# Two-layer diffusion block on one core: the Fourier and gate stage with VectorE in program order

## The chip, the cores and the metric

The kernel runs on one NeuronCore of one Trainium2 chip. The metric is device time in microseconds of one execution. Five engines work in parallel: TensorE (PE in the profile; PEld is its weight load), VectorE (DVE), ScalarE (ACT), GpSimd (POOL) and SyncE (SP), whose queue issues most of the DMAs. Each engine runs its own instructions in order and waits on semaphores for the others.

## The reference, cut to what matters

The input is 1024 latent tokens of width 1024 and 256 context tokens. Layer 0 (the even layer) computes a modulated RMSNorm `h`, one combined projection, and from it two mixers side by side: four Fourier channel groups and four heads of differential attention. Both are multiplied by a SiLU gate and go through one output projection. Layer 1 is a gated short convolution. Shift, scale and gate of each layer are the adaLN columns `silu(c) @ ada_w + ada_b`.

```python
def fourier_mix(u):
    u32 = u.reshape(b, n, F_GROUPS, F_CH).astype(jnp.float32)
    f = jnp.fft.fftn(u32, axes=(1, 3), norm="ortho").real
    return f.reshape(b, n, F_WIDTH)

proj = h @ w_in                       # F | Q | K | V | G
y = concatenate([fourier_mix(proj[F]), rms_norm(attn_o) * (1 - lam_init)]) * silu(proj[G:])
x_lat = x_lat + gate * (y @ w_out)
```

## The kernel before, in words

Every matmul that needs fp32 accuracy is run as three: each operand is split into a rounded part `hi` and a rest `lo`, and hi x hi, hi x lo and lo x hi are summed. ScalarE rounds (`nc.scalar.copy`), VectorE or GpSimd subtracts (function `part`, lines 61 and 62).

**Who sets the order.** A kernel written in this way has its instructions ordered by a planner ahead of time. Inside `manual_schedule(engines={...})` the engines named keep the order of the program text; the others are placed by the planner, which follows the text as a priority and starts an instruction early when its inputs and its buffer are there. From line 555 on only TensorE is in text order; VectorE, ScalarE, GpSimd and the SP queue are the planner's. Tiles come from pools: tiles with the same tag share `bufs` buffers. In the pool `post`, the tag "o" has four buffers and serves `vo` (line 606), `ko` (line 327) and the running sums `ada_sum` (line 564).

**The projections, lines 593 to 660.** `proj_tok(tt, c)` makes one tile of 128 tokens x 512 columns with 24 matmuls of 512 columns. The loops run over K (c = 0), V (c = 1, ten tiles, tt = 0 to 9), Q (c = 2, eight tiles, tt = 2 to 9) and three of the Fourier tiles (c = 3). In this text V3 is the V tile with tt = 3, and so on. Each Q tile is post-processed by `qk_norm`, `qk_scaled` and `qk_a`: a square on ScalarE (L307), a sum on VectorE (L309), two small instructions on GpSimd (L310, L311), then VectorE: `kn` (L316), the two halves of `ko` (L332), L334 and `od` (L340). `od` is transposed by TensorE inside a later tile.

**The adaLN columns beside them.** Eight columns (two of layer 0, six of layer 1) are made in this phase; the text calls them sum 1 to sum 8. `ada_m(half)` takes four 128 x 512 blocks of weights of one half and adds them, each scaled by silu(c), to `ada_sum`: half 0 allocates the sum, and asks for the next column's two loads of 1 MB into three buffers; half 1 finishes it and puts it on the list `sums`. All eight steps of a sum are one chain, each reading what the one before wrote. In the V loop all steps are VectorE's (L579 for the first, L576 for the others). In the Q loop the last two of each half are scaled by ScalarE (L573) and added by GpSimd (L574). `ada_step(n)` takes the latest entry off `sums` when n is odd, and its four matmuls with a column of ones (L586) run in the next `proj_tok` ahead of its last step, k = 7. TensorE is in order, so it waits there for the sum. In the V loop half 0 is called at even tt and half 1 at odd tt; in the Q loop the same. Sum 6 is begun after Q2, finished after Q3 and used in Q5; sums 7 and 8 follow two tiles apart.

**The Fourier stage, lines 664 to 766.** The 512 Fourier columns of the eight token tiles are folded by sums and differences (lines 689 to 705, VectorE), split into the big tiles `arena` (lines 706 to 708), and transformed over tokens per channel group g by `fft_a(g)` (lines 720 to 743: 30 matmuls, then three splits on ScalarE and VectorE) and over channels by `fft_b(g)` (lines 745 to 765: 9 matmuls, a copy `mid`, a copy `fee`, a sum and a difference into `fo`).

**The gates, lines 788 to 911.** The first two gate columns are made by `gate_half(f, half)`, a full tile of 24 matmuls. The other six are made two at a time (groups g = 0, 1, 2) with seven products instead of eight (Strassen's scheme, in Winograd's form): `gop(g, p)` prepares the weight operand, `gate_product(g, p)` runs 12 matmuls into one of the PSUM banks X, Y, Z. Products 5, 6 and 4 need sums and differences of the tokens: `g_diff` (lines 837 to 842) makes `tk[k] = H1[k] - H0[k]` in three steps, `g_less` subtracts it again, `t3` makes H1[k] - H1[k+4]. Of the four k of each, three are VectorE's and one GpSimd's (`GE`, line 854). Product 7 adds onto the bank that product 6 filled, and product 4 onto that of 7, each after ScalarE has copied the bank out.

The text order before is: gate tile (0,1), `fft_a(0)`, then three times [gate tile, `fft_b`, `fft_a`], the products (0,1) and (1,1), the last `fft_b`, then 19 products in the list `order`. Attention follows: its loads into `arena` wait for products 5 and 6 of group 2, and its first score matmul (L982) takes over the PSUM banks of the last products.

Of the kernel before, what the change touches and what calls it, by code (L numbers as in the profile page):

```python
# [8 lines left out]
F32 = mybir.dt.float32  # L9
# [28 lines left out]
def block_kernel(tc, A):  # L38
# [550 lines left out]
    def ada_step(n):  # L589
        if n % 2 and sums:  # L590
            cols.append(lambda a=sums.pop(): ada_c(*a))
# [87 lines left out]
    fx = opn("fx", "right")  # L679


    for n in range(2):
        eo = []
        for m in (n, n + 2):
            psa = pf.pop(0) if pf else proj_tok(NTC + m, 3)
            a = fx.tile([P, NB], F32, name="fa", bufs=1)
            nc.scalar.copy(out=a, in_=psa)
            psb = pf.pop(0) if pf else proj_tok(NTC + m + 4, 3)
            for i, op in enumerate((ALU.add, ALU.subtract)):
                e = fx.tile([P, NB], F32, name=f"fe{i}", bufs=2)  # L690
                nc.vector.tensor_tensor(out=e, in0=a, in1=psb, op=op)
                eo.append(e)
        ea, oa, eb, ob = eo
# [12 lines left out]
        for (h, l), u in zip(EO, us):  # L706
            nc.scalar.copy(out=h[:, n, :], in_=u)
            nc.vector.tensor_sub(out=l[:, n, :], in0=u, in1=f32(h[:, n, :]))
    cls("fx")
# [35 lines left out]
    def fft_b(g, ch, cl, sh, sl, dh, dl):  # L745
# [4 lines left out]
        for pp, a, b, i, n in ((p6, dh, dl, 0, 2), (pe, ch, cl, 0, NB), (po, sh, sl, 2, NB)):  # L750
# [37 lines left out]
    def gate_half(f, half):  # L788
# [7 lines left out]
        gate_out(f, half, ge.tile([P, NB], F32, name="sg", bufs=2), ps)  # L796
# [15 lines left out]
    def gate_product(g, p):  # L812
# [6 lines left out]
        new = lambda: go.tile([P, NB], F32, name="go", bufs=5) if go else ge.tile([P, NB], F32, name="sg", bufs=2)  # L819
# [15 lines left out]
    tk = []  # L835

    def g_diff(t, k, a, b, eng):

        x, y = H[a][k[0]], H[b][k[1]]
        tt = lambda i, j, op: eng.tensor_tensor(out=t, in0=i, in1=f32(j), op=op)  # L840
        tt(f32(x[0]), y[0], ALU.subtract)
        tt(t, x[1], ALU.add)
        tt(t, y[1], ALU.subtract)

    def g_less(k, half, eng):
# [8 lines left out]
    GE = (nc.vector, nc.vector, nc.vector, nc.gpsimd)  # L854
    def t3():
        for k in range(4):
            u = v0[:, hsl[k % 2]]
            g_diff(u, (k, k + 4), 1, 1, GE[k])
            nc.scalar.copy(out=H[1][k][0], in_=u)
            GE[k].tensor_tensor(out=H[1][k][1], in0=u, in1=f32(H[1][k][0]), op=ALU.subtract)  # L860

# [3 lines left out]
    for i in range(2):  # L865
        tk += halves(wp.tile([P, T], F32, name="tk", tag="wraw", bufs=2))
    for k in range(4):
        g_diff(tk[k], (k, k), 1, 0, GE[k])
# [12 lines left out]
    gate_product(1, 1)  # L881
    fft_b(*cur)
# [3 lines left out]
    qs = [quarter_of(t) for t in (*arena, t4)]  # L886
    GB.update({5: [(q[:, 0, :], q[:, 1, :]) for q in qs[0]], 6: [(q[:, 0, :], q[:, 1, :]) for q in qs[1]],
               4: [(q[:, 0, :], q[:, 1, :]) for q in qs[2]]})
    for k in range(4):
        part(tk[k], qs[0][k], GE[k])  # L890
    gop(0, 6)
    for k in range(4):
        g_less(k, 1, GE[k])
        part(tk[k], qs[1][k], GE[k])
    gop(0, 2)
    gop(0, 7)
    gop(1, 5)
    for k in range(4):
        g_less(k, 0, GE[k])
        part(tk[k], qs[2][k], GE[k])  # L900
    order = [(0, 5), (0, 6), (0, 2), (0, 7), (1, 5), (0, 4), (1, 6), (0, 3), (1, 7), (1, 2),
             (2, 1), (1, 4), (2, 5), (2, 6), (1, 3), (2, 7), (2, 2), (2, 4), (2, 3)]
    ahead = order[5:]
    for n, (g, p) in enumerate(order):
        if ahead:
# [4 lines left out]
        gate_product(g, p)  # L910
# [706 lines left out]
```

## Time and profile before

| | |
|---|---|
| three runs, us | 1132.86, 1139.51, 1139.52 (median 1139.51) |
| the profiled execution, us | 1135.15 |
| its span, us | 1133.4 |
| mean granted TensorE clock | 0.974 of full speed |
| projections K, V, Q and Fourier tiles on TensorE | about 23 to 279.7 us |
| Fourier and gate stage on TensorE | 279.7 to 396.6 us |

Times in the views are microseconds from the start of the span. A row of the timeline gives start, duration, engine, line, operation, output <- inputs, shapes and count; in brackets, how long the engine had been idle before it and which instruction ended that. The view of windows gives, for stretches of the span, the busy time of each engine, the mean granted clock of TensorE, and the DMA share. The busy time of a matmul is longer at a lower clock, so idle time and clock both have to be counted.

### The profile page before, as it was taken

To read this page: it belongs to the slowest core of one execution; us is meant where nothing else is said; L and a number is where in the kernel's file an instruction comes from. 1 tells how busy PE (TensorE), PEld (TensorE's weight loads), DVE (VectorE), ACT (ScalarE), POOL (GpSimd) and SP (SyncE) were. 2 spreads that over 40 slices of the span, in tenths; PEclk is the share of its full clock that TensorE was granted. 3 is DMA by queue.
4 is the path that set the end of the run, shared out by engine and by line. 5 is a ranking of instruction groups with operands and counts; after the bars stand their busy time and mean duration, and the time that the engine had idled before them with its cause. 6 is when DMAs were issued, how large, how long until landed. Compare 5 with 4: busy or idle time off the path is not lost.

```text
span 1133.4 us, 14135 instructions
## 1 busy us (share of the span) xinstructions
PE 1043.9 (92%) x5118; PEld 851.1 (75%) x5118; DVE 763.0 (67%) x1073; ACT 480.0 (42%) x868; POOL 498.8 (44%) x422
## 2 busy tenths in 40 slices
PE   4989899989888989999999998889999999998598
PEld 2657688778777878999988876568888888776486
DVE  4599856874868178888873287985645554578642
ACT  4453123311443367777763363633333333343320
POOL 1257103631556236676575455654343444332331
PEclk9999899989899999999999999989999999999799
DMA  9724895434020795271004541121111111111421
GB/s 346 295 94 131 267 296 182 145 112 159 9 93 26 181 262 133 79 182 47 21 20 165 198 165 50 37 75 38 67 46 56 56 57 56 56 67 55 166 76 65
DMA packets 61381, 131.12 MB, mean 116 GB/s; under 512 B 5248, under 2 KB 30208, under 8 KB 58112
## 3 DMA queue, kind: packets, MB, share of 16 engines
q1 hardware_dynamic: 60240, 125.64, 34.8%
q0 software_dynamic: 1072, 4.59, 1.1%
q8 instruction: 40, 0.66, 0.2%
q14 instruction: 29, 0.24, 0.1%
HBM read 105.57 MB, written 24.64 MB: 115 GB/s over the span
## 4 chain that ended last, share of the span: by engine, by line
PE 54%; DVE 16%; POOL 3%; ACT 3%; issue 3%; DMA 3%; SPq 0%; ACTq 0%; DVEq 0%; POOLq 0%
PE psX L649 6%; PE psX L650 6%; PE psX L651 6%; PE ps_av L1032 5%; PE psY L649 3%; PE psY L650 3%; PE psY L651 3%; PE S L982 3%; PE S L983 2%; PE ps_t L1022 2%; DVE nm L987 2%; PE ps_feat L1085 2%; PE ps_feat L1087 2%; PE ps_feat L1086 2%; DVE arena L62 2%
## 5 line engine op out<-in xcount | busy, mean ns | idle before, releaser
L61 ACT CAST wop<-wraw 128x512 fp32r<-128x512 f32 x152 | 93.3, 620 | 130.6 <-PE psY L651 28.0
L62 POOL TENSOR_TENSOR wop<-wraw,wop 128x512 fp32r<-128x512 f32 x72 | 99.7, 1388 | 76.8 <-ACT wop L61 76.4
L284 PE MATMUL ps_tok<-whi,hhi 128*128 128x512 f32 x288 | 119.0, 413 | 3.4 <-ACT hhi L393 2.5
L285 PE MATMUL ps_tok<-whi,hlo 128*128 128x512 f32 x288 | 115.7, 402 | 4.3 <-DVE hlo L397 4.2
L286 PE MATMUL ps_tok<-wlo,hhi 128*128 128x512 f32 x288 | 114.8, 399 | 0.0
L987 DVE TENSOR_REDUCE nm<-S 128x1 f32<-128x1280 f32 x64 | 95.0, 1487 | 22.1 <-PE S L983 20.0
L649 PE MATMUL psX<-B,wop 128*128 128x512 f32 x240 | 97.3, 405 | 9.8 <-ACT c L1293 4.9
L998 ACT ACTIVATE p<-S,nm 128x1280 f32<-128x1280 f32 x64 | 85.2, 1332 | 44.6 <-DVE nm L987 38.9
L650 PE MATMUL psX<-B,wop 128*128 128x512 f32 x240 | 96.9, 404 | 1.5 <-POOL B L1439 1.1
L651 PE MATMUL psX<-B,wop 128*128 128x512 f32 x240 | 96.4, 402 | 0.5 <-POOL wop L62 0.5
L628 POOL TENSOR_TENSOR s<-wraw 128x512 f32<-128x512 f32 x20 | 27.3, 1363 | 120.0 <-DMA wraw<-in_wodd_dram 114.0
L62 DVE TENSOR_TENSOR wop<-wraw,wop 128x512 fp32r<-128x512 f32 x80 | 68.9, 863 | 13.2 <-ACT wop L61 12.9
L628 POOL TENSOR_TENSOR wraw<-wraw 128x512 f32<-128x512 f32 x40 | 56.6, 1421 | 47.9 <-DVE wop L62 40.4
L1032 PE MATMUL ps_av<-v,aT 128*128 128x128 f32 x640 | 76.8, 275 | 0.0
L1032 PEld LDWEIGHTS ps_av<-v,aT 128*128 128x128 f32 x640 | 74.2, 192 | 0.2
L285 PEld LDWEIGHTS ps_tok<-whi,hlo 128*128 128x128 f32 x288 | 55.5, 193 | 18.8 <-DVE hlo L397 8.0
L1009 POOL TENSOR_TENSOR p<-p,cc 128x256 f32<-128x256 f32 x32 | 40.4, 1262 | 65.6 <-DVE cc L1006 46.6
L284 PEld LDWEIGHTS ps_tok<-whi,hhi 128*128 128x128 f32 x288 | 55.7, 193 | 17.8 <-ACT hhi L393 3.7
L649 PE MATMUL psY<-B,wop 128*128 128x512 f32 x160 | 64.1, 400 | 3.6 <-DVE u L1301 1.8
L650 PE MATMUL psY<-B,wop 128*128 128x512 f32 x160 | 64.2, 401 | 0.6 <-POOL B L1439 0.3
L286 PEld LDWEIGHTS ps_tok<-wlo,hhi 128*128 128x128 f32 x288 | 55.4, 192 | 11.9
L651 PE MATMUL psY<-B,wop 128*128 128x512 f32 x160 | 63.7, 398 | 0.0
(344 smaller groups left out, 2671.7 us busy)
## 6 DMA issues: line engine op xcount, KB each, us to landing
ada_raw<-in_ada_dram SPq DMA_DIRECT2D x24, 1024.0 KB, 6.6
wraw<-in_wodd_dram SPq DMA_DIRECT2D x32, 512.0 KB, 3.5
wraw<-in_wo_dram SPq DMA_DIRECT2D x24, 512.0 KB, 3.8
wraw<-in_wtok_dram SPq DMA_DIRECT2D x16, 512.0 KB, 4.2
arena<-kd SPq DMA_DIRECT2D x16, 320.0 KB, 8.6
kq<-kd SPq DMA_DIRECT2D x16, 320.0 KB, 9.7
xt<-in_xT_dram SPq DMA_DIRECT2D x16, 256.0 KB, 5.8
xr<-in_xT_dram SPq DMA_DIRECT2D x16, 256.0 KB, 3.8
```

The lines of the kernel that those rows point to most:

```text
L61: nc.scalar.copy(out=o[:, 0, :], in_=src)
L62: eng.tensor_tensor(out=o[:, 1, :], in0=src, in1=f32(o[:, 0, :]), op=ALU.subtract)
L284: nc.tensor.matmul(ps, lhsT=hh, rhs=whi, start=k == 0, stop=False)
L285: nc.tensor.matmul(ps, lhsT=hl, rhs=whi, start=False, stop=False)
L286: nc.tensor.matmul(ps, lhsT=hh, rhs=wlo, start=False, stop=k == KT - 1)
L628: tt = lambda out, x, y, op: nc.gpsimd.tensor_tensor(out=out, in0=x, in1=y, op=op)
L649: nc.tensor.matmul(ps, lhsT=a, rhs=x[k][0], start=start and k == 0, stop=False, skip_group_check=not start)
L650: nc.tensor.matmul(ps, lhsT=a, rhs=x[k][1], start=False, stop=False, skip_group_check=not start)
L651: nc.tensor.matmul(ps, lhsT=b, rhs=x[k][0], start=False, stop=k == 3, skip_group_check=not start)
L987: nc.vector.tensor_reduce(out=nm, in_=S[m][:, :NKEY], op=ALU.max, axis=AX.X, negate=True)
L998: nc.scalar.activation(out=p, in_=S[m][:, :NKEY], func=AF.Exp, bias=tiles.pop((i, m, "nm")), accum_out=z)
L1032: nc.tensor.matmul(ps, lhsT=groups[i, k // 4][:, (k % 4) * P:(k % 4 + 1) * P], rhs=v[:, k * P:(k + 1) * P], start=k == 0, stop=k == NK - 1)
```

## The change

1. **The order of VectorE.** After the third Fourier tile of the projections the `manual_schedule` is closed and opened again with TensorE and VectorE. So in the whole Fourier and gate stage VectorE runs in text order, and the text is rearranged for that: roundings on ScalarE run one step ahead of the subtractions on VectorE (`lagged`).
2. **Token differences on VectorE alone.** `g_diff`, `g_less`, `t3` and the splits of the `tk` lose their engine argument; GpSimd's quarter of them goes to VectorE. The `tk` differences move to the head of the stage, between the Fourier tiles.
3. **Two gate tiles ahead of the first transform.** (0,1) and (1,1) come before `fft_a(0)`; the remaining two gate tiles and the two first products lie between the transforms.
4. **Products reordered,** so that a product that adds onto a bank seldom follows directly on the one that is copied out of it; operands are prepared four products ahead, after the product, where it was five, ahead of it.
5. **Buffers.** `fa` and `fee` use halves of `v0`; `mid` is copied by ScalarE; the tag "sg" has three buffers instead of two, and odd steps of `t3` use the tag "s1".
6. **The adaLN columns one tile later.** In the V loop `ada_m` begins at tt = 1 with half 0, so halves 0 fall on odd tt; the Q loop continues with half 1 of sum 5 at tt = 2. `ada_step` now takes a sum when its argument is even, and the Q loop calls it with tt + 1. Followed through by hand, sums 1, 2 and 3 are used in V4, V6 and V8 (before: V3, V5, V7). Sums 5 to 8 are still used in Q3, Q5, Q7 and Q9. Sum 6 is begun after Q3 and finished after Q4 (before: after Q2 and Q3), sums 7 and 8 likewise one tile later. Sum 4 stays on the list until the second Fourier tile (before: V9).

```diff
     def ada_step(n):
-        if n % 2 and sums:
+        if n % 2 == 0 and sums:
             cols.append(lambda a=sums.pop(): ada_c(*a))
...
         ps = proj_tok(tt, 1, (4,))
-        ada_m(tt % 2)
+        if tt:
+            ada_m((tt + 1) % 2)
...
-        ada_step(tt)
+        ada_step(tt + 1)
         fins.append(qk_a(proj_tok(tt, 2, (5,)), 0, tt))
-        ada_m(tt % 2, 2)
+        ada_m((tt + 1) % 2, 2)
...
     pf = []
-    ada_step(1)
     for m in (0, 4, 2):
         qk_b(*fins.pop(0))
+        if m == 4:
+            ada_step(0)
         pf.append(proj_tok(NTC + m, 3, (5,)))
...
+    man.__exit__(None, None, None)
+    man = tc.manual_schedule(engines={ENG.PE, ENG.DVE})
+    man.__enter__()
...
+            if m == 1:
+                g_diff(tk[2], (2, 2), 1, 0)
+                g_diff(tk[3], (3, 3), 1, 0)
...
+        if n == 0:
+            g_diff(tk[0], (0, 0), 1, 0)
+            g_diff(tk[1], (1, 1), 1, 0)
...
             if n == 2:
-                nc.vector.tensor_copy(out=mid, in_=p6[:, 0:2])
-        e = fev.tile([P, NB], F32, name="fee", bufs=1)
+                nc.scalar.copy(out=mid, in_=p6[:, 0:2])
+        e = v0[:, 0:NB]
...
     gate_half(0, 1)
+    gate_half(1, 1)
+    t3((0, 1))
     cur = fft_a(0)
-    for g, fh in ((1, (1, 1)), (2, (0, 0)), (3, (1, 0))):
-        gate_half(*fh)
-        fft_b(*cur)
-        cur = fft_a(g)
-        if g == 1:
-            t3()
-            gop(0, 1)
-            gop(1, 1)
-            gop(0, 5)
+    t3((2, 3))
+    gate_half(0, 0)
+    gop(0, 1)
+    gop(1, 1)
+    fft_b(*cur)
+    cur = fft_a(1)
+    gate_half(1, 0)
+    gop(0, 5)
+    gop(0, 2)
+    fft_b(*cur)
+    cur = fft_a(2)
     gate_product(0, 1)
+    gop(1, 5)
+    fft_b(*cur)
+    cur = fft_a(3)
     gate_product(1, 1)
+    gop(1, 2)
+    qs = [quarter_of(t) for t in arena]
+    tpart(qs[0], range(4))
     fft_b(*cur)
...
-    order = [(0, 5), (0, 6), (0, 2), (0, 7), (1, 5), (0, 4), (1, 6), (0, 3), (1, 7), (1, 2),
-             (2, 1), (1, 4), (2, 5), (2, 6), (1, 3), (2, 7), (2, 2), (2, 4), (2, 3)]
-    ahead = order[5:]
+    tpart(qs[1], range(4), 1)
+    order = [(0, 5), (0, 2), (1, 5), (1, 2), (0, 6), (1, 6), (0, 7), (1, 7), (0, 4), (0, 3), (1, 4), (1, 3),
+             (2, 1), (2, 5), (2, 6), (2, 2), (2, 7), (2, 4), (2, 3)]
+    ahead = order[4:]
     for n, (g, p) in enumerate(order):
+        gate_product(g, p)
+        if n in (2, 3):
+            tpart(qs[2], (2 * n - 4, 2 * n - 3), 0)
         if ahead:
             q = ahead.pop(0)
             gop(*q)
             if q[1] == 3:
                 gload(q[0] + 2)
-        gate_product(g, p)
```

`tpart(q, ks, half)` does for each k: `g_less` if a half is given (two subtractions), the rounding on ScalarE, and one step later the subtraction of the rest on VectorE.

More of the change, by code (lines that the diff above doesn't have):

```diff
@@ L679, in block_kernel, with g_diff @@
     fx = opn("fx", "right")
+    tk = []
+    for i in range(2):
+        tk += halves(wp.tile([P, T], F32, name="tk", tag="wraw", bufs=2))
+    def g_diff(t, k, a, b):
+        x, y = H[a][k[0]], H[b][k[1]]
+        tt = lambda i, j, op: nc.vector.tensor_tensor(out=t, in0=i, in1=f32(j), op=op)
+        tt(f32(x[0]), y[0], ALU.subtract)
+        tt(t, x[1], ALU.add)
+        tt(t, y[1], ALU.subtract)
     for n in range(2):
@@ L685, in block_kernel @@
             psa = pf.pop(0) if pf else proj_tok(NTC + m, 3)
-            a = fx.tile([P, NB], F32, name="fa", bufs=1)
+            a = v0[:, NB:T]
             nc.scalar.copy(out=a, in_=psa)
@@ L795, in gate_half @@
             nc.tensor.matmul(ps, lhsT=b, rhs=H[half][k][0], start=False, stop=k == KT - 1)
-        gate_out(f, half, ge.tile([P, NB], F32, name="sg", bufs=2), ps)
+        gate_out(f, half, ge.tile([P, NB], F32, name="sg", bufs=3), ps)
     graws, gops, gdone, gbanks, gouts = {}, {}, set(), {}, {}
@@ L818, in gate_product @@
         f = 2 + 2 * g
-        new = lambda: go.tile([P, NB], F32, name="go", bufs=5) if go else ge.tile([P, NB], F32, name="sg", bufs=2)
+        new = lambda: go.tile([P, NB], F32, name="go", bufs=5) if go else ge.tile([P, NB], F32, name="sg", bufs=3)
         if p in (1, 6):
@@ L833, in gate_product, with g_less @@
             gate_out(f + 1, 0, new(), X)
[L835 to L845, printed above, removed]
+    def g_less(k, half):
         x = H[half][k + 4]
-        eng.tensor_tensor(out=tk[k], in0=f32(x[0]), in1=tk[k], op=ALU.subtract)
-        eng.tensor_tensor(out=tk[k], in0=tk[k], in1=f32(x[1]), op=ALU.add)
+        nc.vector.tensor_tensor(out=tk[k], in0=f32(x[0]), in1=tk[k], op=ALU.subtract)
+        nc.vector.tensor_tensor(out=tk[k], in0=tk[k], in1=f32(x[1]), op=ALU.add)
     def quarter_of(t):
@@ L853, in block_kernel, with lagged, rounded, rest @@
     GB = {1: H[0][:4], 2: H[0][4:], 3: H[1][4:], 7: H[1][:4]}
[L854 to L860, printed above, removed]
+    def lagged(steps):
+        held = None
+        for a, b in steps:
+            r = a()
+            if held:
+                held()
+            held = lambda b=b, r=r: b(r)
+        held()
+    def rounded(src, hi):
+        nc.scalar.copy(out=hi, in_=src)
+    def rest(src, hi, lo):
+        nc.vector.tensor_tensor(out=lo, in0=src, in1=f32(hi), op=ALU.subtract)
+    def t3(ks):
+        def a(k):
+            u = ge.tile([P, NB], F32, name="s1", bufs=1) if k % 2 else v0[:, NB:T]
+            g_diff(u, (k, k + 4), 1, 1)
+            rounded(u, H[1][k][0])
+            return u
+        lagged([(lambda k=k: a(k), lambda u, k=k: rest(u, *H[1][k])) for k in ks])
+    def tpart(q, ks, half=None):
+        def a(k):
+            if half is not None:
+                g_less(k, half)
+            rounded(tk[k], q[k][:, 0, :])
+        lagged([(lambda k=k: a(k), lambda _, k=k: rest(tk[k], q[k][:, 0, :], q[k][:, 1, :])) for k in ks])
     go = None
@@ L864, in block_kernel @@
     gload(1)
[L865 to L868, printed above, removed]
     gate_half(0, 1)
+    gate_half(1, 1)
+    t3((0, 1))
     cur = fft_a(0)
-    for g, fh in ((1, (1, 1)), (2, (0, 0)), (3, (1, 0))):
-        gate_half(*fh)
-        fft_b(*cur)
-        cur = fft_a(g)
-        if g == 1:
-            t3()
-            gop(0, 1)
-            gop(1, 1)
-            gop(0, 5)
+    t3((2, 3))
[9 more added lines that the diff above has]
+    cur = fft_a(2)
     gate_product(0, 1)
+    gop(1, 5)
+    fft_b(*cur)
+    cur = fft_a(3)
     gate_product(1, 1)
+    gop(1, 2)
+    qs = [quarter_of(t) for t in arena]
+    tpart(qs[0], range(4))
     fft_b(*cur)
@@ L885, in block_kernel @@
     t4 = go.tile([P, 8 * NB], F32R, name="t4")
[L886 to L900, printed above, removed]
-    order = [(0, 5), (0, 6), (0, 2), (0, 7), (1, 5), (0, 4), (1, 6), (0, 3), (1, 7), (1, 2),
-             (2, 1), (1, 4), (2, 5), (2, 6), (1, 3), (2, 7), (2, 2), (2, 4), (2, 3)]
-    ahead = order[5:]
+    qs.append(quarter_of(t4))
+    for p, q in zip((5, 6, 4), qs):
+        GB[p] = [(t[:, 0, :], t[:, 1, :]) for t in q]
+    tpart(qs[1], range(4), 1)
+    order = [(0, 5), (0, 2), (1, 5), (1, 2), (0, 6), (1, 6), (0, 7), (1, 7), (0, 4), (0, 3), (1, 4), (1, 3),
+             (2, 1), (2, 5), (2, 6), (2, 2), (2, 7), (2, 4), (2, 3)]
+    ahead = order[4:]
     for n, (g, p) in enumerate(order):
+        gate_product(g, p)
+        if n in (2, 3):
+            tpart(qs[2], (2 * n - 4, 2 * n - 3), 0)
         if ahead:
```

## The prediction

> **What bounds the kernel now.** I read the first part of the page, then the waits of TensorE from 100 to 400 us (the stretch that the change touches), then the windows around each wait.
>
> ```profile
> PE 1043.9 (92%) x5118; PEld 851.1 (75%) x5118; DVE 763.0 (67%) x1073; ACT 480.0 (42%) x868; POOL 498.8 (44%) x422
> ```
> ```profile
> PE ps_col L586 <- POOL ada_sum L574: 6.7, 1, 6.7
> PE ps_col L586 <- DVE ada_sum L576: 4.6, 1, 4.6
> PE ps_gc L732 <- DVE arena L708: 4.5, 2, 3.5
> PE ps_fo L751 <- ACT fee L757: 3.3, 1, 3.3
> PE psX L649 <- ACT go L822: 2.2, 1, 2.2
> PE psX L650 <- DVE arena L62: 0.8, 1, 0.8
> ```
> ```profile
> 129.50:144.70 15.20, 10.62 (x42) 8.87 (x42) 11.45 (x18) 1.25 (x3) 0.00 (x0) 0.78 1.01 364
> 224.10:236.00 11.90, 5.16 (x18) 4.47 (x18) 11.87 (x17) 2.59 (x3) 6.12 (x4) 0.71 0.44 132
> 279.70:296.00 16.30, 11.83 (x56) 10.39 (x55) 16.02 (x16) 6.88 (x13) 9.64 (x6) 0.82 0.22 81
> 328.30:352.40 24.10, 17.80 (x72) 13.66 (x72) 24.02 (x26) 8.79 (x17) 15.07 (x10) 0.93 0.00 2
> ```
>
> TensorE is busy for 92% of the span, so the kernel can only gain where it waits. In this stretch it waits in four places. Columns of the windows: length, busy us of PE, PEld, DVE, ACT, POOL, then the granted clock. The cost of a place is its idle time plus what the low clock adds, busy time x (1 - clock):
> - V loop, sum 1: 4.58 + 10.62 x 0.22 = **6.9 us**
> - Q loop, sum 8: 6.74 + 5.16 x 0.29 = **8.2 us**
> - first transform: 4.47 + 11.83 x 0.18 = **6.6 us**
> - last transform and first products: 6.3 + 17.80 x 0.07 = **7.5 us**
>
> That is 29.2 us, the most this change can bring. The first two have nothing to do with the Fourier stage: they hang on when an adaLN sum is ready, which part 6 of the change moves.
>
> **Term 1, the V loop: -6.9.**
>
> ```profile
> 132.57 2.86 DVE L576 SCALAR_TENSOR_TENSOR ada_sum<-ada_raw,cs,ada_sum 128x512 f32<-128x512 f32 x4 [1.40 <-DMA ada_raw<-in_ada_dram]
> ```
>
> TensorE wanted sum 1 at 129.5 (window above) and had it at 134.1: its last steps stood on VectorE among those of sum 2, which waited for a load until 132.57. After the change sum 1 is wanted in V4, one tile and a column later: TensorE would be there at about 129.5 + 0.7 + 5.2 = 135.4 without a wait. So even with sum 1 as late as now the wait is gone. Bounds: 0 (the planner weaves the chains so that sum 1 is a tile later too) to -6.9. I take -6.9, since the load that delays it isn't on the way of sum 1 itself.
>
> **Term 2, the Q loop: +12.1.** Here the change takes slack away. A sum cannot begin when it likes:
>
> ```profile
> 158.53 0.46 SPq L111 DMA_DIRECT2D ada_raw<-in_ada_dram  x1
> ada_raw<-in_ada_dram SPq DMA_DIRECT2D x24, 1024.0 KB, 6.6
> 184.90 0.69 DVE L316 TENSOR_TENSOR kn<-ps_tok,s 128x512 f32<-128x512 f32 x1 [2.04 <-POOL s L311]
> 185.63 0.76 DVE L332 TENSOR_TENSOR ko<-kn,gt 128x256 f32<-128x256 f32 x2
> 186.31 0.48 DVE L579 TENSOR_SCALAR ada_sum<-ada_raw,cs 128x512 f32<-128x512 f32 x1
> 200.33 0.76 DVE L332 TENSOR_TENSOR ko<-kn,gt 128x256 f32<-128x256 f32 x2
> 201.01 0.48 DVE L579 TENSOR_SCALAR ada_sum<-ada_raw,cs 128x512 f32<-128x512 f32 x1
> 214.43 0.75 DVE L332 TENSOR_TENSOR ko<-kn,gt 128x256 f32<-128x256 f32 x2
> 215.10 0.48 DVE L579 TENSOR_SCALAR ada_sum<-ada_raw,cs 128x512 f32<-128x512 f32 x1
> ```
>
> By my count back from the last of the loads, the first half of sum 6 was asked for at 158.53 and there at about 165. VectorE was idle for 2.04 us until 184.90, yet sum 6 began at 186.31, straight behind `ko`, the tile allocated just ahead of it under the same tag; so did sums 7 and 8. I read this as buffers of one tag being given out in text order. After the change, sums 6, 7 and 8 stand behind the `ko` of Q3, Q5 and Q7 instead of Q2, Q4 and Q6, and are still wanted in Q5, Q7 and Q9.
>
> ```profile
> 181.54 0.60 ACT L307 ACTIVATE sqk<-ps_tok 128x512 f32<-128x512 f32 x1 [1.20 <-PE ps_tok L286]
> 187.90 0.60 ACT L307 ACTIVATE sqk<-ps_tok 128x512 f32<-128x512 f32 x1 [5.76 <-PE ps_tok L286]
> 193.37 0.60 ACT L307 ACTIVATE sqk<-ps_tok 128x512 f32<-128x512 f32 x1 [4.87 <-PE ps_tok L286]
> 200.18 0.60 ACT L307 ACTIVATE sqk<-ps_tok 128x512 f32<-128x512 f32 x1 [1.20 <-PE ps_tok L286]
> 213.23 0.60 ACT L307 ACTIVATE sqk<-ps_tok 128x512 f32<-128x512 f32 x1
> 193.93 2.74 POOL L574 TENSOR_TENSOR ada_sum<-ada_sum,ada_raw 128x512 f32<-128x512 f32 x2
> 209.71 1.36 POOL L574 TENSOR_TENSOR ada_sum<-ada_sum,ada_raw 128x512 f32<-128x512 f32 x1
> 227.15 3.66 POOL L574 TENSOR_TENSOR ada_sum<-ada_sum,ada_raw 128x512 f32<-128x512 f32 x2 [0.43 <-issue]
> 198.40 0.95 PE L586 MATMUL ps_col<-ones,ada_sum 128*128 128x1 f32 x8
> 211.12 1.05 PE L586 MATMUL ps_col<-ones,ada_sum 128*128 128x1 f32 x8
> 230.86 1.44 PE L586 MATMUL ps_col<-ones,ada_sum 128*128 128x1 f32 x6 [6.74 <-POOL ada_sum L574]
> ```
>
> The squares (L307) mark the ends of Q2, Q3, Q4, Q5 and Q7. From the end of a tile to the start of the sum: 186.31 - 181.54 = 4.8 us for Q2, 201.01 - 193.37 = 7.6 for Q4, where another sum's GpSimd work stood in between. The chain itself: 10.4 (186.31 to 196.67), 10.1 (to 211.07), 15.7 (to 230.81). Now sums 6 and 7 have 198.40 - 181.54 = 16.9 and 211.12 - 193.37 = 17.8 and just make it (sum 7 ends at 211.07, its column starts at 211.12). One tile less leaves 198.40 - 187.90 = 10.5, 211.12 - 200.18 = 10.9 and (230.86 - 6.74) - 213.23 = 10.9. Needed are 4.8 + 10.4 = 15.2; I take the short 4.8, because TensorE will have waited for the sum before, so that VectorE and GpSimd are free when the tile ends. Waits: 15.2 - 10.5 = 4.7 in Q5, 4.8 + 10.1 - 10.9 = 4.0 in Q7, and 15.2 - 10.9 = 4.3 in Q9, to which I add 1.3, a quarter of the way to the long chain of sum 8. That is 14.3 us idle, and about 2 us of low clock each (1.5 and 2.3 in the two windows above): 20.3 instead of 8.2, so +12.1. Bounds: -8.2 (no wait at all) to +24.5 (the long values, rival 2). The columns' matmuls (0.95 each) are moved, not saved. What is queued behind a waiting column on TensorE is one step of the tile, so everything after slides by the wait. The loads move with the sums; their buffers come free when a sum's step has read them, and they have a whole tile more.
>
> [...]
>
> **Term 3, the first transform: -6.6.**
>
> ```profile
> 279.67 0.39 PE L793 MATMUL ps_feat<-hhi,whi 128*128 128x512 f32 x1
> 285.12 0.28 PE L730 MATMUL ps_gc<-tabs,arena 128*128 128x256 f32 x1
> 279.98 0.69 DVE L62 TENSOR_TENSOR gop<-graw,gop 128x512 fp32r<-128x512 f32 x1 [9.71 <-ACT gop L61]
> 280.59 1.28 DVE L691 TENSOR_TENSOR fe<-fa,ps_tok 128x512 f32<-128x512 f32 x2
> 285.79 1.75 DVE L62 TENSOR_TENSOR gop<-graw,gop 128x512 fp32r<-128x512 f32 x1
> 288.07 0.68 DVE L62 TENSOR_TENSOR gop<-s,gop 128x512 fp32r<-128x512 f32 x1
> ```
>
> A gate tile is 285.12 - 279.67 = 5.45 us. The planner put operand splits among the folds, and GpSimd's work slowed VectorE: the same split takes 0.68 us alone and 1.75 beside a GpSimd instruction. In text order the folds stand alone: 2 + 4 + 4 instructions at 0.6 each from 279.9, done at 286. The second gate tile holds TensorE until 279.67 + 2 x 5.45 = 290.6, so 4.6 us are spare. If that cover failed, each microsecond past it would be a wait. The 12 steps of `tk` (7.2 us) go into holes such as the 9.71 us before 279.98; the 16 of `t3` (9.6 us) lie beside gate tiles. Nine and twelve of these were VectorE's already.
>
> **Term 4, the last transform and the products: -4.9.**
>
> ```profile
> 377.18 0.39 PE L649 MATMUL psY<-arena,gop 128*128 128x512 f32 x1
> 379.98 0.39 PE L649 MATMUL psX<-arena,gop 128*128 128x512 f32 x1
> ```
>
> The 7.5 us of waits come from `mid` and `fee` behind other work and from a product behind its own copy; copying `mid` on ScalarE and the new order take them away. Two things come back. Product (2,4) now follows directly on (2,7), whose bank ScalarE must copy first: between 0.6 (what ScalarE takes for such a tile, as L307 above) and 2.2 (the wait for L822, with ScalarE late); I take +0.9, nearer to the first, as ScalarE then has little else. And VectorE in order has to do, between the end of `fft_a(3)` and product (0,6): splits until 1.8, one operand, four rests (to 4.8), `fo` (to 6.2), 12 steps for product 6 and one operand (to 14.0 at 0.6 each). With 2.8 us a product (379.98 - 377.18) and 1.75 for `fft_b`, a value of mine from the repeat of the cycle, (0,6) starts at 2.8 + 1.75 + 4 x 2.8 = 15.8. That leaves 1.8; three GpSimd instructions in that time add 3 x 1.07 = 3.2 by the two splits above: +1.4, with 0.3 for small waits at the `fft_b`. Bounds -7.5 to +4.7 (rival 3).
>
> [...]
>
> Buffers ("sg", `v0`) and ScalarE's extra copies I cost at nothing: GpSimd and ScalarE have room (42% and 44% busy). Product 6 of group 2 ends 4 products before attention, 11.2 us, where it was 14; its loads for attention have that as cover, and without it attention would start late by what they lack.
>
> **Sum.** -6.9 + 12.1 - 6.6 - 4.9 = **-6.3 us**: the profiled execution's own 1135.15 (1.75 more than its span) becomes 1128.9. It lies between the runs shown (1132.86 to 1139.52, median 4.4 above it), so I add 1 here and in the rivals' times and forecast **1130**.
>
> **Rivals.**
> 1. *The sums run ahead after all* (the order behind `ko` was the planner's choice, not a rule): no wait in Q, term 2 is -8.2, the sum -26.6, time 1110. For it: sum 5 could run early, and the loads are there. Against: three sums out of three start behind `ko`.
> 2. *Slower: the ladder in Q at its long rows.* Start 7.6 us after the tile, chains of 10.4, 10.1 and 15.7: waits of 7.5, 6.8 and 12.4, with clock 32.7, net +24.5, the sum +6.1, time 1142. It turns the sign from 26.6 us of cost in Q on, 6.9 of idle per wait. For it: those are the rows of Q4 and of sum 8. Against: the waits themselves clear the queues.
> 3. *VectorE in order becomes the bound of the products:* all 12 steps meet GpSimd, 12 x 1.07 = 12.8, less 1.8 spare = 11.0 wait; term 4 is +4.7, the sum +3.3, time 1139. For it: in the window from 328.3 VectorE was busy for 24.02 of 24.10. Against: GpSimd's token work, part of that, is gone.
>
> **Chances.** Forecast 0.55, rival 1 0.2, rival 2 0.15, rival 3 0.1. The forecast's own range is 1121 to 1137; the range to the cases on both sides is 1108 to 1141. About 1% (11 us) is what a measurement of this kernel tells from no change. Faster by more: rival 1 and a quarter of the forecast, 0.36. Slower by more: a part of rival 2, 0.09. The rest, 0.55, is within it.
>
> **What would show it.** Right: no wait of L586 in V; waits of 3 to 6 us of L586 on L574 in Q5, Q7 and Q9, with L579 straight behind the L332 of Q3, Q5 and Q7; no wait of L732 on L708; one of about 0.9 at (2,4). Wrong: sums 6 to 8 beginning before those tiles' `ko`, columns without a wait, or VectorE still behind when (0,6) is due.

## The result, and the profile after

The kernel after takes 1128.59 us (median of 7 runs, 1128.41 to 1131.68), the kernel before 1137.35 (7 runs): the ratio is 0.9931, with a 95% interval of 0.9915 to 0.9948. That is 0.7% faster, within the 1% that the prediction called no change to be told; 1130 was forecast. The profiled execution took 1129.21 with a span of 1127.4, 6.0 less than the span before; the sum of the terms said -6.3.

The first part of the page of after, and the waits of TensorE from 100 to 400 us (total, times, longest):

```profile
PE 1043.6 (93%) x5118; PEld 851.2 (75%) x5118; DVE 755.4 (67%) x1081; ACT 482.2 (43%) x874; POOL 476.7 (42%) x410
```
```profile
PE ps_col L586 <- POOL ada_sum L574: 13.7, 3, 5.6
PE psX L652 <- DVE gop L62: 2.2, 1, 2.2
...
PE S L1020 <- DMA arena<-kd: 0.7, 1, 0.7
PE psX L650 <- ACT go L852: 0.7, 1, 0.7
PE ps_fo L774 <- ACT mid L778: 0.3, 1, 0.3
```

TensorE's busy time is the same as before, to 0.3 us; only its idle time moved. The waits on the folds (4.5), on `fee` (3.3) and on the product behind its own copy (2.2) are gone, and so is the wait of the V loop. Three waits for a sum of the Q loop stand in their place. The windows of after are those of the V loop, of the first transform, and of the last transform with the first products (length, busy us of PE, PEld, DVE, ACT, POOL, then clock, DMA share, GB/s):

```profile
129.50:144.70 15.20, 15.20 (x76) 12.75 (x75) 12.62 (x20) 2.94 (x5) 0.00 (x0) 1.00 1.02 347
284.40:299.00 14.60, 14.60 (x80) 12.72 (x79) 12.33 (x19) 7.39 (x13) 0.00 (x0) 1.00 0.25 95
330.00:352.40 22.40, 19.90 (x80) 15.49 (x79) 22.07 (x28) 8.75 (x17) 8.64 (x7) 0.92 0.12 42
```

The V loop and the first transform run without idle time at full clock (1.00). What is lost in Q is seen better in two wide windows, first of before, then of after:

```profile
165.00:210.00 45.00, 45.00 (x218) 37.66 (x217) 32.06 (x54) 15.69 (x23) 18.02 (x17) 1.00 0.59 196
210.00:250.00 40.00, 33.26 (x153) 27.28 (x152) 34.25 (x49) 9.96 (x14) 22.54 (x15) 0.91 0.35 104
```
```profile
165.00:210.00 45.00, 39.37 (x175) 32.48 (x174) 29.18 (x47) 14.26 (x21) 19.22 (x17) 0.92 0.52 172
210.00:250.00 40.00, 31.90 (x143) 26.01 (x141) 28.75 (x40) 10.64 (x15) 16.63 (x14) 0.87 0.36 105
```

Idle plus busy time x (1 - clock): before 0 and 6.74 + 33.26 x 0.09 = 9.7; after 5.63 + 39.37 x 0.08 = 8.8 and 8.10 + 31.90 x 0.13 = 12.2. So Q costs 21.0 where it cost 9.7.

Two points of time split the whole. Here are the first gate matmul and the first scores of attention, of before and then of after:

```profile
279.67 0.39 PE L793 MATMUL ps_feat<-hhi,whi 128*128 128x512 f32 x1
397.48 0.50 PE L982 MATMUL S<-arena 128*128 128x512 f32 x1 [0.78 <-DMA sgd<-go]
```
```profile
284.40 0.39 PE L816 MATMUL ps_feat<-hhi,whi 128*128 128x512 f32 x1
391.86 0.47 PE L1019 MATMUL S<-arena 128*128 128x512 f32 x1 [0.83 <-issue]
```

Up to the first gate tile, after is 4.7 us late. From there to attention it takes 107.5 us instead of 117.8: 10.3 gained. The end comes 6.0 earlier.

The rows of a Q sum in after (the last matmul of Q3, the square of Q3 and what ScalarE did just ahead of it, the last `ko` half and the first step of sum 6, its column in Q5):

```profile
179.49 0.40 PE L286 MATMUL ps_tok<-wlo,hhi 128*128 128x512 f32 x1
180.60 1.34 ACT L573 ACTIVATE ada_raw<-ada_raw,cs 128x512 f32<-128x512 f32 x2 [4.58 <-DVE od L340]
181.85 0.58 ACT L307 ACTIVATE sqk<-ps_tok 128x512 f32<-128x512 f32 x1
...
185.91 0.76 DVE L332 TENSOR_TENSOR ko<-kn,gt 128x256 f32<-128x256 f32 x2
186.59 0.48 DVE L579 TENSOR_SCALAR ada_sum<-ada_raw,cs 128x512 f32<-128x512 f32 x1
...
196.22 1.86 PE L586 MATMUL ps_col<-ones,ada_sum 128*128 128x1 f32 x8 [5.63 <-POOL ada_sum L574]
```

The sum starts straight behind the `ko` of Q3, 4.7 us after the square, and its chain of 9.6 us ends at 196.2. The tile itself ends at 179.89, 6.7 us ahead of the sum's start: here the square doesn't mark the end of the tile, since it stands on ScalarE behind an L573 that started late.

### The profile page after: what moved, and what is told of

Read it like the earlier page. It is cut to its first block, busy times and chain, and to the rows that moved or that the text cites. A ratio compares the mean times of both kernels' runs of the same rounds, so it can differ in the third digit from the quotient of the medians.

```text
span 1127.4 us, 14123 instructions
## 1 busy us (share of the span) xinstructions
PE 1043.6 (93%) x5118; PEld 851.2 (75%) x5118; DVE 755.4 (67%) x1081; ACT 482.2 (43%) x874; POOL 476.7 (42%) x410
## 4 chain that ended last, share of the span: by engine, by line
PE 56%; DVE 15%; ACT 4%; issue 2%; POOL 2%; ACTq 0%; DVEq 0%; POOLq 0%
PE psX L650 6%; PE psX L652 6%; PE psX L651 6%; PE ps_av L1069 5%; PE psY L650 3%; PE psY L651 3%; PE psY L652 3%; PE S L1019 3%; PE S L1020 2%; DVE nm L1024 2%; PE ps_t L1059 2%; PE ps_feat L1122 2%; PE ps_feat L1123 2%; PE ps_feat L1124 2%; PE ps_tok L284 1%
## 5 line engine op out<-in xcount | busy, mean ns | idle before, releaser
L62 DVE TENSOR_TENSOR wop<-wraw,wop 128x512 fp32r<-128x512 f32 x80 | 65.7, 823 | 13.2 <-ACT wop L61 13.0
L286 PEld LDWEIGHTS ps_tok<-wlo,hhi 128*128 128x128 f32 x288 | 55.8, 194 | 12.1
```

Of the source, the lines that this page charges most:

```text
L62: eng.tensor_tensor(out=o[:, 1, :], in0=src, in1=f32(o[:, 0, :]), op=ALU.subtract)
L286: nc.tensor.matmul(ps, lhsT=hh, rhs=wlo, start=False, stop=k == KT - 1)
```

## Experiments

The theory: the change consists of two parts that have nothing to do with each other. The stage gains about 10 us, and the adaLN part gives V's 6.9 back but loses some 12 in Q, because a sum starts only behind the `ko` allocated ahead of it. All ratios below are to the kernel before, with 95% intervals. "Stretch" is the time from the first gate matmul to the first scores, as above.

**1. The adaLN part alone.** The kernel before with these lines of after:

```diff
-        if n % 2 and sums:
+        if n % 2 == 0 and sums:
...
-        ada_m(tt % 2)
+        if tt:
+            ada_m((tt + 1) % 2)
...
-        ada_step(tt)
+        ada_step(tt + 1)
...
-        ada_m(tt % 2, 2)
+        ada_m((tt + 1) % 2, 2)
...
     pf = []
-    ada_step(1)
     for m in (0, 4, 2):
         qk_b(*fins.pop(0))
+        if m == 4:
+            ada_step(0)
```

> The kernel before with part 6 alone (columns a tile later, sums a tile later). My theory: this part costs time. No wait of TensorE for a sum in V (-6.9), and three waits of 3 to 6 us in Q5, Q7 and Q9, 13 to 15 us idle in all and some 6 us of low clock (+12.1 net of the 8.2 that go), the waits of the Fourier stage unchanged: 4 to 6 us slower than before, ratio about 1.004. Rival A: the Q waits come from the stage's own edits by way of the planner, so that here none is seen: 15 us faster than before, ratio about 0.987. Rival B: the waits are taken back later, ratio 1.000.

Measured: 1141.66 us, ratio 1.0067 (1.0037 to 1.0097), span 1137.7, 4.3 more than before. Its waits:

```profile
PE ps_col L586 <- POOL ada_sum L574: 12.7, 3, 5.1
PE ps_gc L734 <- DVE arena L710: 4.4, 2, 3.3
```

There is no wait in V, there are three in Q, and the stage is as before (stretch 117.7; on the folds 4.4 us of wait, and the waits on `fee` and on the product's copy are 3.3 and 2.2 again). Both rivals fall: this part is a loss by itself.

**2. The stage alone.** The kernel after with the sums and columns of before (the lines of experiment 1 the other way round).

> The kernel after with the sums and columns of before. My theory: the two parts add up. The waits of before in V (4.6) and Q (6.7) are back, the three new Q waits are gone, and the Fourier stage keeps its gain of some 10 us: about 10.5 us faster than before and 4.7 faster than after, ratio to before about 0.991 - 0.996 x 4.7/1128 = 0.987 to 0.990. Rival: the parts do not add (VectorE's new order changes what is free for the sums), and the time is that of after, ratio 0.993.

Measured: 1123.68 us, ratio 0.9913 (0.9888 to 0.9937), span 1123.1. The stretch is 107.4, as in after, and the waits for sums are those of before:

```profile
PE ps_col L586 <- POOL ada_sum L574: 6.9, 2, 6.7
PE ps_col L586 <- DVE ada_sum L576: 4.5, 1, 4.5
```

The spans add: -10.3 here and +4.3 in experiment 1 make -6.0, which is after's. The timed ratio is above the expected 0.987 to 0.990, and the product of the two, 0.998, is half a per cent above after's 0.9931, a little more than the intervals allow. Part of it may lie in the kernel before, whose median was 1134.73 in the session of these two runs and 1137.35 beside after; against 1134.73, after's ratio would be 0.9946. Nor is the exact agreement of the spans more than chance: in this run the first gate tile comes at 281.99, 2.3 us later than in before though the text ahead of it is before's, and another 2.2 us are gained behind the first scores, where all these kernels have the same text. So two single executions are compared to about 2 us, no better; the rest stays open.

**3. What holds a sum back.** In the kernel after, the text of each sum of Q is put ahead of the tile's `ko`; the columns stay.

```diff
         ada_step(tt + 1)
+        ada_m((tt + 1) % 2, 2)
         fins.append(qk_a(proj_tok(tt, 2, (5,)), 0, tt))
-        ada_m((tt + 1) % 2, 2)
```

> The kernel after with each sum's text moved ahead of the Q tile's ko instead of behind it; columns unchanged. Theory (the sum starts straight behind the last allocation of its tag in the text): sums 6 to 8 now start straight behind the ko of Q2, Q4 and Q6, one tile earlier, where they have 16.9 us or more for a chain of 15: no wait in Q5 and Q7, 0 to 6.7 us in Q9, so 10 to 20 us faster than after, 1109 to 1118. Rival (the sum starts when the planner finds VectorE free, or when its load is there): start times and waits as in after, 1128.

Measured: 1118.8 us, ratio 0.9863 (0.9835 to 0.9892), 0.7% better than after and just above the expected range. The waits for sums in Q fall from 13.7 to 8.1. Sum 6 in this kernel:

```profile
180.12 0.76 DVE L332 TENSOR_TENSOR ko<-kn,gt 128x256 f32<-128x256 f32 x2
180.79 0.48 DVE L579 TENSOR_SCALAR ada_sum<-ada_raw,cs 128x512 f32<-128x512 f32 x1
```

The sum again starts straight behind a `ko`, but behind that of Q2, and its row shows no wait for a load. So the start follows the text, as the theory has it; the rival falls. The columns wait 1.25, 1.41 and 5.42 us: slightly more than expected in Q5 and Q7, and in Q9 sum 8 takes its 15.7 us of before, beside the splits of the gate weights on VectorE. That the common tag is the reason, and not the place in the text alone, this run doesn't tell apart; a sum in a tag of its own was not run.

**4. The oldest sum first.** In after, so that sums 5 to 8 are each used two tiles later:

```diff
-            cols.append(lambda a=sums.pop(): ada_c(*a))
+            cols.append(lambda a=sums.pop(0): ada_c(*a))
```

> The kernel after with the oldest finished sum used first, so that each sum of the Q loop has two more tiles before its column. Theory: lateness of the sums is all that stands in Q; the three waits (13.7 us idle, some 6 us of clock) vanish: 1107 to 1112. Rival: two finished sums then lie in the four buffers of their tag all the time, a ko has to wait for a column to free one, and the waits come back on the transposes of Q: 1120 or more.

Measured: 1119.78 us, ratio 0.9877 (0.985 to 0.9903). Both accounts hold in part:

```profile
PE ps_t L349 <- DVE od L340: 5.6, 2, 4.4
PE ps_t L349 <- DVE tl L353: 2.8, 2, 1.4
PE ps_col L586 <- POOL ada_sum L574: 1.7, 1, 1.7
```

Waits for sums fall from 13.7 to 1.7, but transposes of Q tiles now wait 8.4 for VectorE's `od` and `tl`, where the rival put the waits. That they come from a lack of buffers, as the rival had it, isn't shown: in the longest one `od` (238.00) stands in VectorE's order behind a `kn` that waited 1.22 us for GpSimd.

**5. Columns a tile later.** In the Q loop of after, for columns in Q2, Q4, Q6, Q8 and the second Fourier tile, with sum 4 first, so that only one finished sum lies in a buffer:

```diff
-        ada_step(tt + 1)
+        ada_step(tt)
```

> The kernel after with the columns of the Q loop in Q2, Q4, Q6, Q8 and F4 instead of Q3, Q5, Q7, Q9 and F4: sum 4 is used first, so that only one finished sum lies in a buffer, and sums 6 to 8 get a tile more. Theory: a sum that starts 4.8 us after the end of its tile and takes 10 to 12.4 us has then some 17 to 18 us, so no column waits in Q: 13.7 us idle and some 6 us of clock less than after, 1107 to 1112, with no new wait of the transposes. Rival (buffers: three sums and the ko do not fit in four): waits of TensorE on od as with the oldest sum first, 1117 or more.

Measured: 1117.88 us, ratio 0.9845 (0.9825 to 0.9865).

```profile
PE ps_t L349 <- DVE od L340: 4.1, 1, 4.1
...
PE ps_col L586 <- POOL ada_sum L574: 2.6, 2, 1.4
```

Better than after by 0.9%, but 1107 to 1112 was expected. The waits for sums are down to 2.6; one transpose waits 4.1 for `od`. So lateness of the sums is not all that stands in Q: with the sums out of the way, VectorE's work on the Q tiles comes late next.

**6. Both: columns later and the text of the sums earlier.** The edits of experiments 5 and 3 in one kernel:

```diff
-        ada_step(tt + 1)
+        ada_step(tt)
+        ada_m((tt + 1) % 2, 2)
         fins.append(qk_a(proj_tok(tt, 2, (5,)), 0, tt))
-        ada_m((tt + 1) % 2, 2)
```

> The kernel after with both edits: columns of the Q loop a tile later, and each sum's text ahead of the tile's ko. By the theory one of the two edits is enough, so this gains nothing over the later columns alone: within 2 us of it. Rival: the sums still wait for something else that their text brings forward, and this is faster than the later columns alone by 3 us or more.

Measured: 1115.01 us, ratio 0.982 (0.9802 to 0.9838); the span, 1113.8, is 3.7 less than with the later columns alone. The time is 2.9 us less, between the 2 us of the theory and the 3 of the rival, and the two intervals overlap. Of the 3.7 us of the spans, 0.9 is there at the first matmul of the projections (22.24 against 23.17), where the edit can't be the reason. The waits in Q are about as long as with the later columns alone: the wait for `od` goes from 4.1 to 2.6, but one of 1.3 for `tl` is new. So the earlier text may be worth something of its own, but this run doesn't show it.

**7. VectorE in program order.** In after, VectorE goes back to the planner in the stage:

```diff
-    man = tc.manual_schedule(engines={ENG.PE, ENG.DVE})
+    man = tc.manual_schedule(engines={ENG.PE})
```

> The kernel after with VectorE left to the planner in the Fourier and gate stage, all else as after. My theory for the first transform: the cover (a second gate tile) does the work, and by the profile of before the planner's folds ended at 288.75, before 290.6, so it still finds no wait there; in the products the order matters little: within 2 us of after. Rival: VectorE's order carries the stage's gain, and waits on the folds, the fo or the token parts come back: 5 us or more slower than after, ratio to before 0.998 or more.

Measured: 1127.1 us, ratio 0.9923 (0.99 to 0.9947): not to be told from after. The first transform has no wait; nor has product (0,6). The stretch is 104.4, 3.1 shorter than in after, and the waits for sums in Q grew from 13.7 to 15.4. Half of the 3.1 us is chance: in experiments 3, 4 and 6 the stage is that of after, and the stretch is 105.9 (the last section has the reason). The order of VectorE, the first point of the change, brings nothing here; in the products it costs 1.5 us by these stretches.

**8. One gate tile ahead of the first transform.** In after:

```diff
-    gate_half(1, 1)
-    t3((0, 1))
     cur = fft_a(0)
+    gate_half(1, 1)
+    t3((0, 1))
```

> The kernel after with one gate tile ahead of the first transform instead of two (the second, with its two differences, right behind the transform). Theory: in the profile after the folds end 3.3 us before the end of the second gate tile; without that tile (5.4 us) they are 2.1 us late: TensorE waits up to 2.1 us for them in the first transform, with low clock 2 to 3.5 us slower than after, ratio to before 0.995 to 0.997. Rival: VectorE in program order alone is enough, no wait and the time of after.

Measured: 1129.29 us, ratio 0.9942 (0.9922 to 0.9963), the span 1126.4; the time isn't to be told from after's. The rival holds, there is no wait:

```profile
292.17 0.28 PE L753 MATMUL ps_gc<-tabs,arena 128*128 128x256 f32 x1
...
293.27 0.68 DVE L728 TENSOR_TENSOR arena<-fe,arena 128x512 fp32r<-128x512 f32 x1
```

The last rest of the folds ends at 293.95, 1.8 us behind the transform's first matmul, as expected; but the transform reads its four inputs one after the other over 3.5 us, and each is there when its turn comes.

**9. Neither cover.** The edits of experiments 7 and 8 together:

```diff
-    man = tc.manual_schedule(engines={ENG.PE, ENG.DVE})
+    man = tc.manual_schedule(engines={ENG.PE})
...
-    gate_half(1, 1)
-    t3((0, 1))
     cur = fft_a(0)
+    gate_half(1, 1)
+    t3((0, 1))
```

> The kernel after with VectorE left to the planner in the stage and one gate tile ahead of the first transform, that is, both edits undone that each were found unneeded alone. Theory: they are two covers for the same wait, so without both it returns: 3 to 5 us idle on the splits of the folds in the first transform, some 2 us of clock, 5 to 7 us slower than after, ratio to before 0.997 to 0.999. Rival: a third edit (the differences out of GpSimd, the buffers in v0) had removed it, no wait there, and the time of after or less.

Measured: 1127.57 us, ratio 0.9914 (0.9891 to 0.9936). My theory fell, the rival holds. The first transform waits 0.7 us, where before it waited 4.5:

```profile
PE ps_gc L755 <- DVE arena L728: 0.7, 1, 0.7
```

In its window, GpSimd does nothing, where in before it was busy for 9.64 of 16.3 us:

```profile
284.00:296.00 12.00, 11.33 (x65) 9.81 (x64) 9.44 (x17) 6.32 (x11) 0.00 (x0) 1.00 0.41 139
```

**10. GpSimd beside the folds.** So a new theory: the operands of the products were GpSimd's work beside the folds, and the change wrote them later in the text. Kernel 9 with three operands moved up:

```diff
     cur = fft_a(0)
+    gop(0, 1)
+    gop(1, 1)
+    gop(0, 5)
...
-    gop(0, 1)
-    gop(1, 1)
...
-    gop(0, 5)
```

> The kernel with both covers undone (planner for VectorE, one gate tile), and the first three operands of the gate products written right behind the first transform, as close to the folds as before had them; the third needs three GpSimd instructions. Theory, formed after that kernel showed a wait of only 0.7 us: what made the first transform wait before was GpSimd's operand work (L628 there) beside the folds and their splits, at some 1.1 us for each VectorE instruction that it met, and the change removed it by writing these operands later. So with it back: splits of 1.7 us instead of 0.6, 3 to 5 us of wait in the first transform, 3 to 6 us slower than without it, ratio to before 0.995 to 0.998. Rival: the wait hung on the token differences or the buffers of before; still 0.7 us, ratio 0.991.

Measured: 1132.73 us, ratio 0.9967 (0.9951 to 0.9983), against 0.9914 without it; the stretch is 111.4 instead of 105.3. The wait is back:

```profile
286.53 1.29 POOL L629 TENSOR_TENSOR s<-graw 128x512 f32<-128x512 f32 x1 [24.51 <-DMA graw<-in_wg_dram]
286.66 3.41 DVE L715 TENSOR_TENSOR v<-fe,fe 128x512 f32<-128x512 f32 x2
289.60 1.61 POOL L629 TENSOR_TENSOR graw<-s,graw 128x512 f32<-128x512 f32 x1
289.99 1.77 DVE L715 TENSOR_TENSOR fe<-fe,fe 128x512 f32<-128x512 f32 x1
292.29 0.68 DVE L715 TENSOR_TENSOR fe<-fe,fe 128x512 f32<-128x512 f32 x1
294.82 0.58 PE L755 MATMUL ps_gc<-tabs,arena 128*128 128x256 f32 x1 [3.60 <-DVE arena L728]
```

A fold that meets GpSimd takes 1.7 to 1.8 us, the one at 292.29 that meets nothing 0.68. Besides, two more operand splits than in experiment 9 stand ahead of the rests on VectorE (0.6 each). Against experiment 9, counted from the first fold, the first rest ends 3.4 us later: the three slowed folds make 3.2 of it, the two splits 1.2, less 0.95 of idle time that is gone. This is the wait of before: when GpSimd's operand runs decides it.

What holds that operand back in the change can be read from GpSimd's first row for it, of before and then of after:

```profile
282.00 1.62 POOL L628 TENSOR_TENSOR s<-graw 128x512 f32<-128x512 f32 x1 [24.91 <-DMA graw<-in_wg_dram]
306.51 1.60 POOL L629 TENSOR_TENSOR s<-graw 128x512 f32<-128x512 f32 x1 [44.72 <-DVE hlo L882]
```

In both texts the operand stands behind `t3`. In before the planner starts it as soon as its load is there, ahead of all of `t3`. In after it waits for L882, the last subtraction of `t3`, which reads `s`: that is the tag "s1" with its one buffer, which part 5 of the change gave to the odd steps of `t3` too. In experiments 7, 8 and 9 as well it starts 0.1 us behind that subtraction (302.14, 309.74 and 303.59). So by these rows it is the shared buffer that keeps GpSimd away from the folds, and experiment 10 took the operand ahead of `t3` in the queue for it. A kernel in which `t3` has another buffer, and nothing else is moved, was not run; what the later place in the text does without the shared buffer stays open.

**11. A token difference back on GpSimd.** The fourth of the differences and its parts, 14 instructions, go back to GpSimd; the text order is after's.

```diff
+    GE = (nc.vector, nc.vector, nc.vector, nc.gpsimd)
...
-        nc.vector.tensor_tensor(out=tk[k], in0=f32(x[0]), in1=tk[k], op=ALU.subtract)
+        GE[k].tensor_tensor(out=tk[k], in0=f32(x[0]), in1=tk[k], op=ALU.subtract)
...
```

> The kernel after with the fourth token difference and its parts (14 instructions) back on GpSimd, the order of the text unchanged. Theory (the prediction's price: a GpSimd instruction beside VectorE costs VectorE 1.07 us, as much as it takes off it): nothing won, and the last part, now on GpSimd at 1.3 us an instruction, comes later: product (0,6) waits 4 to 6 us instead of 2.2, 2 to 6 us slower than after, ratio to before 0.995 to 0.998. Rival: VectorE was the bound of the products and is relieved of some 9 us: the 2.2 us wait goes, 2 to 3 us faster than after.

Measured: 1132.07 us, ratio 0.9947 (0.9929 to 0.9965); the stretch is 110.9 instead of 107.5.

```profile
PE ps_col L586 <- POOL ada_sum L574: 17.0, 3, 8.8
PE psX L652 <- DVE gop L62: 3.9, 1, 3.9
```

The wait of (0,6) is 3.9 instead of 2.2, and the waits in Q grew as well, by 3.3, which the edit does not explain. The rival falls, and the forecast made with the prediction's price came out: taking this work off GpSimd was worth some 3 us in the stage of this execution. By the times alone, the intervals of this kernel and of after overlap.

**12. The best of these.** The edits of experiments 6 and 7 together: columns later, sums earlier in the text, VectorE the planner's:

```diff
-        ada_step(tt + 1)
+        ada_step(tt)
+        ada_m((tt + 1) % 2, 2)
         fins.append(qk_a(proj_tok(tt, 2, (5,)), 0, tt))
-        ada_m((tt + 1) % 2, 2)
...
-    man = tc.manual_schedule(engines={ENG.PE, ENG.DVE})
+    man = tc.manual_schedule(engines={ENG.PE})
```

> The kernel after with three edits: columns of the Q loop in Q2 to Q8 and F4, each sum's text ahead of the tile's ko, and VectorE left to the planner in the stage. From the profiles: the first two give a span of 1113.8, and the third took 3.1 us off the stretch from the first gate tile to the first scores of attention (107.5 to 104.4). If these add: span 1110 to 1111, 1112 in time, ratio to before 0.979. Rival: the planner, which now places VectorE in the whole stretch, moves the sums again (with it alone the Q waits grew from 13.7 to 15.4 us): 1114 to 1118.

Measured: 1112.76 us, ratio 0.9787 (0.9764 to 0.981), span 1109.9: as expected, 2.1% faster than before and, by the two ratios, 1.4% faster than after. The stretch is 104.3 (105.9 in experiment 6), and the two longest waits that are left in Q are these:

```profile
PE ps_t L349 <- DVE od L340: 2.6, 1, 2.6
PE ps_col L586 <- POOL ada_sum L574: 2.4, 1, 2.4
```

## Why the prediction was right, and where it was not

**Term 1, the V loop (-6.9): right.** The window has no idle time at clock 1.00; the column came at 135.88, 135.4 was worked out.

**Term 2, the Q loop (+12.1): right in mechanism and size.** By the wide windows it is 21.0 - 9.7 = +11.3, and by the late first gate tile 4.7 + 6.9 = +11.6. The sums start 4.7, 4.8 and 4.8 us after the squares of their tiles (4.8 was taken), with chains of 9.6, 10.1 and 12.4 (10.4, 10.1 and 11.7 taken). The single waits were less well hit: 5.6, 2.7 and 5.4 against 4.7, 4.0 and 5.6. Two things failed there. The prediction took squares for the ends of tiles; the square of Q3 came 2.0 us after the end, behind ScalarE's L573, so sum 6 started 6.7 us after the end of its tile. The time that the tile leaves was as forecast: 196.22 - 5.63 - 179.89 = 10.7 us, against 10.5. Sums 7 and 8, on the other hand, were wanted 12.3 and 11.8 us after their squares, not 10.9, since behind the wait before TensorE still ran at half speed (granted clock 0.53), until 202.1 and 219.1. By luck the errors of the waits cancel to 0.6. Experiment 3 showed that a sum's start goes with its text, and experiment 1 that this part needs nothing of the stage.

**Term 3, the first transform (-6.6): right in size, wrong in the reason.** The wait and the low clock went (0.82 before, 1.00 after). But the step that put it down to folds that "in text order stand alone" and to a second gate tile as cover failed: each can be undone without a wait, and without both it is 0.7 us. The half of the step that held is the other one, that GpSimd's work slows VectorE (1.7 to 1.8 us for a fold beside it, 0.68 for one without): experiment 10 brought the wait back with three operands written earlier. What kept GpSimd away was by its rows the shared "s1", a buffer that the prediction did not look at. The spare time was also reckoned wrongly. It is 3.3 us, not 4.6 (the folds end at 292.0, since the rests waited 0.91 us for ScalarE), and it isn't needed, since the transform takes its inputs one at a time.

**Term 4, the last transform and the products (-4.9): mis-sized.** The copies that were waited for are gone, and the wait at (2,4) is 0.73 (0.9 was taken). But (0,6) waits 2.2 us, and with 0.3 at `fft_b` and the clock the window costs 2.5 + 19.90 x 0.08 = 4.1: with (2,4) 4.8 is left of 7.5, a gain of 2.7. Of the 2.2 us that are missing, 0.8 is the term of +1.4 for VectorE being late, which was too small, and 1.6 is the low clock behind that wait, for which the sum had no term at all. In experiments 3, 4, 6 and 8 the same wait had no low clock behind it, so this second part is chance. The price was right: in after three GpSimd instructions in that time make three of VectorE's take 1.67, 1.79 and 1.78 us instead of 0.68, which is 3.2 in all as forecast. Experiment 7 names what makes VectorE late: with the planner's order that wait is gone. Rival 3, VectorE in order as the bound, was thus true in kind, at 2.2 us and not 11. Which of the reordered products, `mid` on ScalarE and the buffers brought how much was not tried one by one.

**What was costed at nothing.** The loads of attention are late by 0.7 us (the wait for kd in the list, which before doesn't have); whether the one product less of cover is the reason was not tried. Nothing is lost by it: the next wait of the scores, for `p`, is 0.89 where it was 1.94, and the end gained 0.4 more than the first scores did. Of the buffers, only "sg" and `v0` were named and costed at nothing; the one that mattered was "s1".

**The sum.** -6.9 + 11.3 - 6.6 - 2.7 = -4.9, against -6.0 of the spans; the 1.1 us between lie outside these windows and are not assigned. That the forecast of -6.3 lies so near is in part luck: term 4 promised 2.2 us too much, term 2 took away 0.8 too much, and the 1.1 fill most of the rest. So the large change moved little because its two halves took from each other: 10.3 us won in the stage, and 4.7 net lost ahead of it, where the sums of Q begin a tile later while their columns in Q5, Q7 and Q9 stay. (One slip in the chances: rival 1 and a quarter of the forecast make 0.34, not 0.36.)

## What to carry to other kernels

When a change shifts a schedule by one place, count for each consumer how much time its producer now has, from the event that releases the producer and not from when its data are there; here that count gave a loss of 12 us within one, with two errors of 1 to 2 us that cancelled. A row that stands for an event, as the square for the end of a tile, can itself be held up on its engine. Undo every part of a change by itself before believing what it is for: the two covers of the first transform, one named in the change's own title, were not needed, and a delay of GpSimd's operand, by its place in the text and a buffer that it now shared, did their work. And when one wait is removed, look for what is late next on the same tiles; after the sums it was VectorE's `od`.

## What the runs showed of the hardware

In these runs a wait of TensorE often cost more than its length, short ones too. Behind the 2.69 us wait in Q7 of after:

```profile
214.57 1.05 PE L586 MATMUL ps_col<-ones,ada_sum 128*128 128x1 f32 x8 [2.69 <-POOL ada_sum L574]
215.48 0.73 PE L284 MATMUL ps_tok<-whi,hhi 128*128 128x512 f32 x1
...
218.56 0.58 PE L285 MATMUL ps_tok<-whi,hlo 128*128 128x512 f32 x1
218.98 0.39 PE L286 MATMUL ps_tok<-wlo,hhi 128*128 128x512 f32 x1
```

The column itself still runs at nearly full speed (1.05 against 0.95 without a wait, and 1.86 behind the waits of 5.4 and 5.6). Then matmuls take 0.63 instead of 0.39 us until 219.1, some 3.5 us at about half speed (granted clock 0.53 from 215.48 to 219.10). Behind the 5.63 us wait in Q5 the column is slow at once, and half speed lasts 5.9 us, to 202.1 (clock 0.50 to 198.1, then 0.53). The 2.22 us wait at 347.15 was followed by such a stretch from 348.7 to 352.2 (0.52); a wait of 2.20 us at the same product in experiment 3 was not: from the second on, its matmuls take 0.39 or 0.40. That is the chance named above: in after and in experiments 2 and 5 this wait has the half speed behind it, and the stretch to the first scores is 107.4 to 107.5; in experiments 3, 4, 6 and 8 it has not, and the stretch is 105.9. The clock of 300 to 400 us is 0.97 in after, 0.98 in experiments 2 and 5 and 1.00 in 3, 4 and 8; in experiment 6 the matmuls behind the wait at 337.19 take 0.39 or 0.40 from the second on.

Two shorter waits, each at a column and with no other of 0.9 us or more in the 8 us ahead of it, had half speed behind them too: 1.37 us (experiment 5, at 198.55, with matmuls of 0.63 from 200.60 on) and 1.41 (experiment 3, at 205.78, the same from 208.30 to 211.49). One of 1.25 (experiment 3, at 191.34) had none. At the first scores of experiment 9, half speed from 395.75 to 399.19 followed three waits of 0.83, 0.77 and 0.94 us within 5.3 us. So the length of the last wait alone does not tell in these runs whether the clock falls: 0.94 was enough there, and 2.20 was not in experiment 3.
